# Attention in a two-layer decoder kernel: how the q and k operands of a head are rounded and placed, and where the norm's square stands

## The chip, the cores and the metric

The kernel runs on one core of a Trainium2 chip. The metric is the device time of one launch in microseconds (us). Five engines execute their own instruction streams in order and wait for one another by semaphores: TensorE (PE) multiplies matrices and transposes, VectorE (DVE) and ScalarE (ACT) do elementwise work and reductions, GpSimd (POOL) and SyncE (SP) are used here almost only to issue DMA transfers. Matmul results land in PSUM, in banks of 128 rows by 512 float32; everything else lies in SBUF.

## The reference

Two identical layers are applied to a residual stream x of 512 tokens by 1024 features, all float32:

```python
x = x + 0.5 * swiglu(rms_norm(x, ffn1_norm[l]), ffn1_w_in[l], ffn1_w_out[l])
h = rms_norm(x, mix_norm[l]) @ w_mix_in[l]
(c_x, c_b, c_c, h_q, h_f, h_i, h_g, f_q, f_k, f_v, f_f) = jnp.split(h, split_at, axis=-1)
y = jnp.concatenate([short_conv_mixer(c_x, c_b, c_c, conv_w[l]),
                     hgrn2_mixer(h_q, h_f, h_i, h_g, lower_bounds[l], hgrn_out_gain[l]),
                     fox_mixer(f_q, f_k, f_v, f_f, fox_f_bias[l], fox_q_gain[l], fox_k_gain[l])], axis=-1)
x = x + y @ w_mix_out[l]
x = x + 0.5 * swiglu(rms_norm(x, ffn2_norm[l]), ffn2_w_in[l], ffn2_w_out[l])
```

The change concerns fox_mixer, an attention of 8 heads of 64 features with normalised queries and keys and a forget term, and the last step of hgrn2_mixer:

```python
qh = rms_norm(heads(q), q_gain) * (HEAD_DIM ** -0.5)
kh = rms_norm(heads(k), k_gain)
cum = jnp.cumsum(jax.nn.log_sigmoid(f_logit + f_bias), axis=1)
s = jnp.einsum('bhqd,bhkd->bhqk', qb, kh) + (cb[..., :, None] - cum[..., None, :])   # causal mask
o = jnp.einsum('bhqk,bhkd->bhqd', softmax(s), vh)                                    # attention
o = rms_norm(o, out_gain) * silu(gate)                                               # end of hgrn2_mixer
```

## The kernel before

Each layer is a feed-forward stage, a mixing stage and a second feed-forward stage. In the feed-forward stages PE works through float32 products in three passes: every operand is split into a rounded high part and the remainder (ACT rounds, lines 311 and 803; DVE subtracts, lines 312 and 805), and lines 322, 330 and 331 multiply high by high, low by high and high by low. The same lines do the dense products of the mixing stage, with weights that SP loads (line 294). "Dense" below means these.

Attention goes head by head, 0 to 3 in the first half and 4 to 7 in the second. Function fox_prep makes the operands of one head. Four transposes bring q (64 rows) and k (64 rows) of the head into one bank. Then it forms four tiles for the score product: QA holds q high in rows 0 to 63 and q low in rows 64 to 127; KA holds k high in both halves; QB holds q high and two rows of ones; KB holds k low and two rows of the forget term. A product over the 128 rows of QA and KA gives high by high and low by high, and a second one over 66 rows of QB and KB gives high by low and the forget term. In the kernel before, ACT rounds q high into QA (line 1563) and k high into KA (line 1564), two transfers on SP copy q high to QB (line 1565) and k high to KA's other half (line 1566), and DVE subtracts to get q low (line 1567) and k low (line 1571), each operation over 64 rows. POOL writes the ones of QB in every call (line 1557). For heads 0 and 1 the transposes go to a bank of the kind "sc" before attention begins, for the others to one of the kind "pt". There are two banks of either kind.

Function fox_attend then walks through four blocks of 128 queries per head, in the order of items (h, i). `LOOK` = 3 items ahead it issues the scores (lines 1586 and 1587, a bank "sc"), DVE reduces them to the negated maximum nm (line 1591), ACT takes the exponential (line 274) and scales by the reciprocal of the sum (line 1597; for the third block DVE does, line 1599). At the item itself PE transposes P into a bank "pt" (line 1651), ACT rounds it to PH (line 1653), DVE forms the rest PL (line 1654), and one item later (`LAG` = 1) PE multiplies by V (line 1609). ACT and DVE then bring the result of a head from its bank "po" to fo (lines 1622 and 1623). The call for the next head's operands stands at the beginning of item (h, 0), so it is one head ahead; the second half is a new call of fox_attend, which begins with the operands of head 4.

Beside attention, PE gets dense work handed out in steps (the function beside in mix): the projections of the second half, the short convolution, then the output projection.

The hgrn2 mixer runs before attention in the same stage. Its final norm leaves a mean of squares in two pt banks. ACT takes Ln and Exp (through line 274) and a Square, and DVE combines this with the banks in two operations (line 1473, in0 = the bank): those are the last readers of the two banks. They stand in the instruction streams beside the first items of attention, whose transposes need the same two banks.

The order of the instructions on each engine isn't the order of the code: a scheduler lays them out by its own estimates and by priorities that rise in the order of the code. `high_priority()` makes the instructions issued within it go ahead of others that could stand at the same place.

Of the kernel before, what the change touches and what calls it, by code (L numbers as in the profile page):

```python
# [8 lines left out]
F32 = mybir.dt.float32  # L9
F32R = mybir.dt.float32r  # L10
# [3 lines left out]
AF = mybir.ActivationFunctionType  # L14
ALU = mybir.AluOpType
# [8 lines left out]
P = 128  # L24
# [20 lines left out]
EPS = 1e-6  # L45
# [3 lines left out]
NH = 8  # L49
# [108 lines left out]
class Trunk:  # L158
# [864 lines left out]
    def mix(self, l, w, w_out, conv_w, out_gain, q_gain, k_gain, f_bias, next_gain):  # L1023
        nc, tc = self.nc, self.tc
        FM2 = [slice(0, P), slice(P, 2 * P)]
        TOK = [slice(c, c + P) for c in (0, 128, 256, 384)]
        with tc.tile_pool(name=self.n("mix"), bufs=1) as mp:
# [10 lines left out]
            og, qkg, fb, cw = col("og", 1), col("qkg", 1), col("fb", NH), col("cw", 6)  # L1038
# [99 lines left out]
            for part, n in enumerate(hgrn):  # L1138
                if n is None:
                    break  # L1140
                if n == 0:
                    left.close()
                    ap1 = left.enter_context(
                        tc.tile_pool(name=self.n("at"), bufs=1, reuse_waits="tile")
                    )
                    for tag in ("PH", "PL"):
                        ap1.tile([P, 4, 2, P], F32R, tag=tag, name=self.n(tag), bufs=2)
                    ops = {h: self.fox_prep(ap1, h, half[0][0], qkg, "sc") for h in range(2)}
                if part < 2:
                    next(decay, None)  # L1150
                for _ in range(n):
                    next(dense, None)
            attend = self.fox_attend(ap1, 0, half[0], qkg, ops)
            next(attend)
            for _ in dense:
                pass
# [27 lines left out]
            def beside(attend, dense, first=0, then=()):  # L1184
                for _ in range(first):
                    next(dense, None)
                for n, _ in enumerate(attend, first):
                    if n == 3 and then:
                        then()
                    if n >= 2:  # L1190
                        next(dense, None)
                for _ in dense:
                    pass
# [23 lines left out]
                        add(2 * dg + i, banks[i])  # L1217

            beside(attend, conv(), 1, finish)
            beside(self.fox_attend(ap1, 1, half[1], qkg, {}), most())  # L1220
            self.ntog = 0
            for dg in range(2):
                banks = self.next4()
# [41 lines left out]
    def hgrn(self, l, hp, hb, z, q, v, sg, og):  # L1265
# [202 lines left out]
        for x in range(2):  # L1468
            self.act(span(r, x), mb[x], AF.Ln, bias=self.epsc)
        self.act(r, r, AF.Exp, scale=-0.5)  # L1470
        self.act(t, r, AF.Square)
        for x in range(2):
            nc.vector.scalar_tensor_tensor(
                out=span(t, x), in0=mb[x], scalar=EPS, in1=span(t, x), op0=ALU.add, op1=ALU.mult
            )
        nc.vector.tensor_scalar(t, t, scalar1=-0.5, scalar2=1.5, op0=ALU.mult, op1=ALU.add)
        nc.vector.tensor_mul(r, r, t)
        nc.vector.tensor_mul(o, o, r)
# [70 lines left out]
                )  # L1549
        half[hf] = qk, V  # L1550

    def fox_prep(self, pool, h, qk, g, tag="pt"):
        nc = self.nc
        tl = lambda p, tag: pool.tile([p, T], F32R, tag=tag, name=self.n(tag), bufs=2)
        QA, QB, KA, KB = tl(P, "QA"), tl(66, "QB"), tl(P, "KA"), tl(66, "KB")
        nc.sync.dma_start(KB[64:66, :].bitcast(F32), self.negc[h : h + 1, :, :].bitcast(F32))
        nc.gpsimd.memset(QB[64:66, :].bitcast(F32), 1.0)
        b = self.bank(tag)
        for i in range(4):
            nc.tensor.transpose(  # L1560
                b[:, i * P : (i + 1) * P], qk[:, i, h % 4].rearrange("p w d -> p (w d)"), self.ident
            )
        nc.scalar.activation(QA[:64, :], b[:64, :], AF.Copy, scale=g[:64, :])
        nc.scalar.activation(KA[64:, :], b[64:, :], AF.Copy, scale=g[64:, :])
        nc.sync.dma_start(QB[:64, :].bitcast(F32), QA[:64, :].bitcast(F32))
        nc.sync.dma_start(KA[:64, :].bitcast(F32), KA[64:, :].bitcast(F32))
        nc.vector.scalar_tensor_tensor(
            out=QA[64:, :], in0=b[:64, :], scalar=g[:64, :], in1=QA[:64, :],
            op0=ALU.mult, op1=ALU.subtract,
        )  # L1570
        nc.vector.scalar_tensor_tensor(
            out=KB[:64, :], in0=b[64:, :], scalar=g[64:, :], in1=KA[64:, :],
            op0=ALU.mult, op1=ALU.subtract,
        )
        return QA, QB, KA, KB

    def fox_attend(self, pool, hf, qkv, g, ops):
        nc = self.nc
        qk, V = qkv
        tl = lambda tag, n: pool.tile([P, T], F32, tag=tag, name=self.n(tag), bufs=n)  # L1580

        def scores(ops, i):
# [46 lines left out]
        late = []  # L1629
        heads = range(4 * hf, 4 * hf + 4)  # L1630
        items = [(h, i) for h in heads for i in range(4)]
        if heads[0] not in ops:
            ops[heads[0]] = self.fox_prep(pool, heads[0], qk, g)
        pb = {it: scores(ops[heads[0]], it[1]) for it in items[:LOOK]}
        for n, (h, i) in enumerate(items):
            yield
            if i == 0 and h + 1 in heads and h + 1 not in ops:
                ops[h + 1] = self.fox_prep(pool, h + 1, qk, g)
            if n + LOOK < len(items):
                h2, i2 = items[n + LOOK]  # L1640
                pb[h2, i2] = scores(ops[h2], i2)
# [10 lines left out]
            t3 = tb.rearrange("p (j t) -> p j t", j=4)[:, : i + 1, :]  # L1652
            nc.scalar.copy(PH[:, : i + 1, i % 2, :], t3)
            nc.vector.tensor_sub(PL[:, : i + 1, i % 2, :], t3, PH[:, : i + 1, i % 2, :])
            if len(late) and n >= late[0][0] + LAG:
                values(*late.pop(0)[1:])
            if i % 2:
# [215 lines left out]
```

## Time and profile before

Three runs took 1806.88, 1807.59 and 1808.02 us.

| | |
|---|---|
| median of the three runs | 1807.59 us |
| profiled execution | 1808.44 us |
| its span | 1806.7 us |
| granted TensorE clock in it | 1.0 |
| instructions in the trace | 34748 |
| attention stage, first layer | about 450 to 590 us of the span |
| attention stage, second layer | about 1340 to 1480 us |
| feed-forward stages | 50 to 340, 590 to 900, 900 to 1240 and 1480 to 1807 us |

A table by stage gives, for a stretch of the span, its length and then the busy time of PE, of PE's weight loads, of DVE, ACT and POOL, each with the number of instructions, then the clock, the share of the DMA engines' time and GB/s. A list of waits names the engine, tile and line that waited, the engine, tile and line that released it, the total in us, the number of times and the longest. A line of the timeline holds start, duration, engine, line, operation, the tiles written and read, and in brackets the idle time of the engine just before it and what ended this. A line on a group gives count, then least, median and greatest duration in ns. PE's instructions overlap: the distance from one start to the next is what one costs.

### The profile page before, as it was taken

The numbers are of one execution on the slowest core, as the hardware profiler recorded it, in microseconds if no ns is written. First come the engines' busy times: TensorE is split into PE (matmuls) and PEld (weight loads), VectorE is DVE, ScalarE is ACT, GpSimd is POOL, SyncE is SP. The second block draws the span as 40 slices with busy tenths as digits, with TensorE's granted clock in tenths as the row PEclk, the third lists the DMA queues.
The fourth block names the chain that finished last, engine by engine and source line by source line (L and its number), as shares of the span: only waits on it lengthen the run. The fifth ranks groups of instructions, "written<-read, shape, count | busy, mean of one in ns | idle before, by whom it ended". The sixth has DMA issues, their size and how long they took to land.

```text
span 1806.7 us, 34748 instructions
## 1 busy us (share of the span) xinstructions
PE 1795.8 (99%) x14267; PEld 1681.3 (93%) x14267; DVE 1453.4 (80%) x2036; ACT 1000.7 (55%) x1437; POOL 170.4 (9%) x172
## 2 busy tenths in 40 slices
PE   9999999999999999999999999999999999999999
PEld 7899999899888899999889999998998888999997
DVE  8889787776887898879679887876868878888893
ACT  5455554464786465556446555555547855555551
POOL 0011120100000001112001111201000000020210
PEclk9999999999999999999999999999999999999999
DMA  7668783233323767868265787823333247687762
GB/s 203 182 142 186 178 178 98 72 79 83 88 74 111 218 140 161 198 160 169 82 205 133 165 189 191 169 66 81 78 89 89 71 138 188 164 159 192 159 134 94
DMA packets 243486, 250.94 MB, mean 139 GB/s; under 512 B 18520, under 2 KB 228192, under 8 KB 243328
## 3 DMA queue, kind: packets, MB, share of 16 engines
q1 hardware_dynamic: 189424, 182.38, 33.8%
q0 software_dynamic: 53600, 66.09, 23.2%
q8 instruction: 112, 1.84, 0.4%
q14 instruction: 46, 0.38, 0.1%
q10 hardware_dynamic: 304, 0.27, 0.0%
HBM read 223.98 MB, written 2.10 MB: 125 GB/s over the span
## 4 chain that ended last, share of the span: by engine, by line
PE 92%; DVE 3%; ACT 3%; issue 1%; DMA 1%; SPq 0%; ACTq 0%; DVEq 0%
PE mm L322 13%; PE mm L330 13%; PE mm L331 13%; PE sc L330 6%; PE sc L331 6%; PE sc L322 6%; PE pt L322 6%; PE pt L330 6%; PE pt L331 6%; PE po L330 4%; PE po L322 4%; PE po L331 4%; ACT hl L311 1%; PE po L1609 1%; PE pt L1651 1%
## 5 line engine op out<-in xcount | busy, mean ns | idle before, releaser
L803 ACT CAST hl<-w 128x1024 fp32r<-128x1024 f32 x322 | 336.7, 1050 | 313.7 <-PE mm L331 82.4
L805 DVE TENSOR_TENSOR hl<-w,hl 128x1024 fp32r<-128x1024 f32 x322 | 392.2, 1221 | 80.7 <-ACT hl L803 80.7
L312 DVE TENSOR_TENSOR hl<-st,hl 128x512 fp32r<-128x512 f32 (+3 forms) x192 | 162.3, 845 | 106.3 <-ACT hl L311 105.5
L311 ACT CAST hl<-st 128x512 fp32r<-128x512 f32 (+3 forms) x192 | 142.6, 743 | 169.9 <-PE po L331 64.6
L322 PE MATMUL mm<-xc,hl 128*128 128x256 f32 (+1 forms) x733 | 201.2, 276 | 0.0
L330 PE MATMUL mm<-xc,hl 128*128 128x256 f32 x728 | 201.2, 276 | 0.0
L331 PE MATMUL mm<-xc,hl 128*128 128x256 f32 x728 | 201.0, 276 | 0.0
L322 PE MATMUL sc<-xc,hl 128*128 128x256 f32 (+1 forms) x532 | 146.0, 276 | 0.0
L330 PE MATMUL sc<-xc,hl 128*128 128x256 f32 x528 | 146.0, 276 | 0.0
L331 PE MATMUL sc<-xc,hl 128*128 128x256 f32 x528 | 145.9, 276 | 0.0
L322 PEld LDWEIGHTS mm<-xc,hl 128*128 128x128 f32 x733 | 137.4, 188 | 0.2
L330 PEld LDWEIGHTS mm<-xc,hl 128*128 128x128 f32 x728 | 136.7, 188 | 0.0
L331 PEld LDWEIGHTS mm<-xc,hl 128*128 128x128 f32 x728 | 136.7, 188 | 0.0
L322 PE MATMUL pt<-xc,hl 128*128 128x256 f32 (+1 forms) x482 | 132.6, 276 | 0.0
L330 PE MATMUL pt<-xc,hl 128*128 128x256 f32 x480 | 132.6, 276 | 0.0
L331 PE MATMUL pt<-xc,hl 128*128 128x256 f32 x480 | 132.5, 276 | 0.0
L322 PE MATMUL mm<-x,hl 128*128 128x512 f32 x272 | 107.4, 395 | 0.0
L331 PE MATMUL mm<-x,hl 128*128 128x512 f32 x272 | 106.4, 391 | 0.0
L330 PE MATMUL mm<-x,hl 128*128 128x512 f32 x272 | 106.1, 390 | 0.0
L322 PEld LDWEIGHTS sc<-xc,hl 128*128 128x128 f32 x532 | 99.7, 188 | 0.2
L331 PEld LDWEIGHTS sc<-xc,hl 128*128 128x128 f32 x528 | 99.1, 188 | 0.1
L330 PEld LDWEIGHTS sc<-xc,hl 128*128 128x128 f32 x528 | 99.2, 188 | 0.0
(513 smaller groups left out, 5594.1 us busy)
## 6 DMA issues: line engine op xcount, KB each, us to landing
w<-in_ffn_w_in_dram SPq DMA_DIRECT2D x140, 512.0 KB
w<-in_ffn_w_out_dram SPq DMA_DIRECT2D x64, 512.0 KB
w<-in_ffn_w_out_dram POOLq DMA_DIRECT2D x56, 512.0 KB, 8.3
st<-in_w_mix_in_dram SPq DMA_DIRECT2D x88, 256.0 KB
st<-in_ffn_w_in_dram SPq DMA_DIRECT2D x70, 256.0 KB
w<-in_ffn_w_in_dram POOLq DMA_DIRECT2D x35, 512.0 KB, 8.5
w<-S POOLq DMA_DIRECT2D x35, 512.0 KB, 4.7
st<-in_ffn_w_out_dram SPq DMA_DIRECT2D x24, 512.0 KB
```

The costliest lines, as they stand in the source:

```text
L311: a = nc.scalar.copy(hi, src[:, c : c + w])
L312: b = nc.vector.tensor_sub(lo, src[:, c : c + w], hi)
L322: i = nc.tensor.matmul(acc[:, c], ah, bh[:, c], start=first and c.start == 0, stop=False, skip_group_check=True,)
L330: nc.tensor.matmul(acc, a, b, start=False, stop=False, skip_group_check=True)
L331: i = nc.tensor.matmul(acc, c, d, start=False, stop=last, skip_group_check=True)
L803: A(nc.scalar.copy(hi, src))
L805: return lambda: V(nc.vector.tensor_sub(lo, src, hi))
L1609: nc.tensor.matmul(self.ob[:, t0 + u * P : t0 + 2 * P], V[:, j, h % 4].rearrange("p a d -> p (a d)"), part[:, j, u:, :].rearrange("p i t - ...
L1651: nc.tensor.transpose(tb[:, j * P : (j + 1) * P], p[:, j * P : (j + 1) * P], self.ident)
```

## The change

It has three parts.

First, fox_prep gets a second form, `ahead=True`, for heads 2 to 7. One ACT operation over all 128 rows rounds the bank into KA (q high in rows 0 to 63, k high in rows 64 to 127), and one DVE operation over 128 rows writes the remainders into QA (q low above, k low below). Four transfers on POOL's queue then place the halves: KA's upper half to QB, QA's lower half to KB, KA's upper half to QA's lower half, and at last KA's lower half to its upper half. To make this so, the order of halves in QA is turned: q low in rows 0 to 63, q high in rows 64 to 127. The third transfer overwrites what the second reads; the fourth overwrites what the first and the third read. Heads 0 and 1 keep the old form.

Second, these operands are made two heads ahead: the call stands behind the rounding of item (h, 0) and is for head h + 2, across the two halves too, so that heads 4 and 5 are prepared in the first half. QB is no longer a new tile per head but one of two lasting ones, whose rows of ones are written once per layer.

Third, the Square of the hgrn norm and the two DVE operations that read the banks stand in `high_priority()`.

PE at the beginning of attention in the first layer. Before: the scores of head 0's last and head 1's first block, the first transpose of P, then dense work.

```order
L1586 MATMUL sc_5471<-KA_5286,QA_5284 128x512
L1587 MATMUL sc_5471<-KB_5287,QB_5285 128x512
L1586 MATMUL sc_5487<-KA_5303,QA_5301 128x128
L1587 MATMUL sc_5487<-KB_5304,QB_5302 128x128
L1651 MATMUL pt_5483<-ident,P_5387 128x128
L322 MATMUL mm_5451<-x_383_3562,hl_5505 128x512
```

PE at the same place after (line 1565 is now the transposes of fox_prep, 1603 and 1604 the scores, 1664 the transposes of P).

```order
L1603 MATMUL sc_5471<-KA_5289,QA_5288 128x512
L1604 MATMUL sc_5471<-KB_5290,QB_5284 128x512
L1664 MATMUL pt_5483<-ident,P_5387 128x128
L1565 MATMUL pt_5491<-ident,qk_4135 128x128 x4
L1603 MATMUL sc_5502<-KA_5304,QA_5303 128x128
L1604 MATMUL sc_5502<-KB_5305,QB_5285 128x128
L322 MATMUL mm_5451<-x_383_3562,hl_5520 128x512
```

The transposes for head 2 now stand directly behind the first transpose of P, and take the second pt bank. The dense matmuls follow behind the scores.

DVE at that place before. T_5544 is the norm's tile, pt_5376 and pt_5377 are its two banks; V is the values' tile of the second half.

```order
L1599 TENSOR_SCALAR P_5407<-P_5407,rs_5406 128x384
L312 TENSOR_TENSOR hl_5573<-st_5570,hl_5573 128x512
L1546 SCALAR_TENSOR_TENSOR V_5246<-mm_5247,invc_3890,V_5246 128x4x64
L1546 SCALAR_TENSOR_TENSOR V_5246<-po_5248,invc_3890,V_5246 128x4x64
L1473 SCALAR_TENSOR_TENSOR T_5544<-pt_5376,T_5544 128x512
L1546 SCALAR_TENSOR_TENSOR V_5246<-mm_5247,invc_3890,V_5246 128x4x64
L312 TENSOR_TENSOR hl_5608<-st_5605,hl_5608 128x512
L1546 SCALAR_TENSOR_TENSOR V_5246<-po_5248,invc_3890,V_5246 128x4x64
L1591 ISA P_5476,nm_5474<-sc_5471,zm_3700 128x512
L1591 ISA nm_5474 128x1
L1654 TENSOR_TENSOR PL_5482<-pt_5483,PH_5481 128x128
L1473 SCALAR_TENSOR_TENSOR T_5544<-pt_5377,T_5544 128x512
```

DVE there after (line 1477 is the former 1473, 1551 the former 1546).

```order
L1612 RECIPROCAL rs_5396<-rs_5396 128x1
L1477 SCALAR_TENSOR_TENSOR T_5559<-pt_5376,T_5559 128x512
L312 TENSOR_TENSOR hl_5588<-st_5585,hl_5588 128x512
L1477 SCALAR_TENSOR_TENSOR T_5559<-pt_5377,T_5559 128x512
L1612 RECIPROCAL rs_5406<-rs_5406 128x1
L1551 SCALAR_TENSOR_TENSOR V_5246<-mm_5247,invc_3890,V_5246 128x4x64
L1616 TENSOR_SCALAR P_5407<-P_5407,rs_5406 128x384
L1551 SCALAR_TENSOR_TENSOR V_5246<-po_5248,invc_3890,V_5246 128x4x64
L312 TENSOR_TENSOR hl_5623<-st_5620,hl_5623 128x512
L1551 SCALAR_TENSOR_TENSOR V_5246<-mm_5247,invc_3890,V_5246 128x4x64
L1608 ISA P_5476,nm_5474<-sc_5471,zm_3700 128x512
```

The two readers of the norm's banks have moved up, ahead of the V operations and the third block's scaling, and only one hl subtraction parts them.

SP around the seam between the halves, before: the transfers of heads 4 and 5 stand between the weight loads (numbers 6064 to 6067 belong to head 4, 6111 to 6114 to head 5).

```order
L294 DMA st_6327<-in_w_mix_out_dram 128x2x256
L294 DMA st_6367<-in_w_mix_out_dram 128x256
L1565 DMA QB_6065<-QA_6064 64x512
L1566 DMA KA_6066<-KA_6066 64x512
L1565 DMA QB_6112<-QA_6111 64x512
L1566 DMA KA_6113<-KA_6113 64x512
L294 DMA st_6399<-in_w_mix_out_dram 128x2x256
```

POOL after, for head 5 (6013 to 6015) and the first of head 6 (6137).

```order
L1578 DMA QB_5285<-KA_6014 64x512
L1578 DMA KB_6015<-QA_6013 64x512
L1578 DMA QA_6013<-KA_6014 64x512
L1578 DMA KA_6014<-KA_6014 64x512
L1578 DMA QB_5284<-KA_6137 64x512
```

The copies have gone from SP to POOL, where nothing else stands between them in this stage.

PE at the seam, after: the last scores of head 4, the transposes of head 6, four dense matmuls, and the first scores of head 5. The transposes of head 5 stand 50 rows ahead of the last two rows.

```order
L1603 MATMUL sc_6120<-KA_5837,QA_5836 128x512
L1604 MATMUL sc_6120<-KB_5838,QB_5284 128x512
L1664 MATMUL pt_6132<-ident,P_6095 128x128
L1565 MATMUL pt_6140<-ident,qk_4812 128x128 x4
L322 MATMUL mm_6166<-cyh_3698,hl_6210 128x512
L330 MATMUL mm_6166<-cyl_6043,hl_6210 128x512
L331 MATMUL mm_6166<-cyh_3698,hl_6210 128x512
L322 MATMUL mm_6167<-cyh_3698,hl_6210 128x512
L1603 MATMUL sc_6151<-KA_6014,QA_6013 128x128
L1604 MATMUL sc_6151<-KB_6015,QB_5285 128x128
```

Before, the operands of heads 4 and 5 were made here, at the seam; now those of head 6 are.

The diff:

```diff
@@ mix
+                    self.qb = pair(ap1, "QB", F32R)
+                    for t in self.qb:
+                        nc.gpsimd.memset(t[64:66, :].bitcast(F32), 1.0)
                     ops = {h: self.fox_prep(ap1, h, half[0][0], qkg, "sc") for h in range(2)}
...
-            attend = self.fox_attend(ap1, 0, half[0], qkg, ops)
+            attend = self.fox_attend(ap1, 0, half, qkg, ops)
...
-            beside(self.fox_attend(ap1, 1, half[1], qkg, {}), most())
+            beside(self.fox_attend(ap1, 1, half, qkg, ops), most())
@@ hgrn
-        self.act(t, r, AF.Square)
-        for x in range(2):
-            nc.vector.scalar_tensor_tensor(
-                out=span(t, x), in0=mb[x], scalar=EPS, in1=span(t, x), op0=ALU.add, op1=ALU.mult
-            )
+        with self.tc.high_priority():
+            self.act(t, r, AF.Square)
+            for x in range(2):
+                nc.vector.scalar_tensor_tensor(
+                    out=span(t, x), in0=mb[x], scalar=EPS, in1=span(t, x),
+                    op0=ALU.add, op1=ALU.mult,
+                )
@@ fox_prep
-    def fox_prep(self, pool, h, qk, g, tag="pt"):
+    def fox_prep(self, pool, h, qk, g, tag="pt", ahead=False):
...
-        QA, QB, KA, KB = tl(P, "QA"), tl(66, "QB"), tl(P, "KA"), tl(66, "KB")
+        QA, KA, KB = tl(P, "QA"), tl(P, "KA"), tl(66, "KB")
+        QB = self.qb[h % 2][:66, :]
         nc.sync.dma_start(KB[64:66, :].bitcast(F32), self.negc[h : h + 1, :, :].bitcast(F32))
-        nc.gpsimd.memset(QB[64:66, :].bitcast(F32), 1.0)
...
+        if ahead:
+            f = lambda a, r=slice(0, 64): a[r, :].bitcast(F32)
+            k = slice(64, P)
+            nc.scalar.activation(KA, b, AF.Copy, scale=g)
+            nc.vector.scalar_tensor_tensor(
+                out=QA, in0=b, scalar=g, in1=KA, op0=ALU.mult, op1=ALU.subtract
+            )
+            for out, src in (
+                (f(QB), f(KA)), (f(KB), f(QA, k)), (f(QA, k), f(KA)), (f(KA), f(KA, k)),
+            ):
+                nc.gpsimd.dma_start(out, src)
+            return QA, QB, KA, KB
@@ fox_attend
-        if heads[0] not in ops:
-            ops[heads[0]] = self.fox_prep(pool, heads[0], qk, g)
...
-            if i == 0 and h + 1 in heads and h + 1 not in ops:
-                ops[h + 1] = self.fox_prep(pool, h + 1, qk, g)
...
             nc.vector.tensor_sub(PL[:, : i + 1, i % 2, :], t3, PH[:, : i + 1, i % 2, :])
+            if i == 0 and h + 2 < NH:
+                ops[h + 2] = self.fox_prep(
+                    pool, h + 2, half[(h + 2) // 4][0], g, ahead=True
+                )
```

More of the change, by code (lines that the diff above doesn't have):

```diff
@@ L1575, in fox_prep, with fox_attend @@
         return QA, QB, KA, KB
-    def fox_attend(self, pool, hf, qkv, g, ops):
+    def fox_attend(self, pool, hf, half, g, ops):
         nc = self.nc
-        qk, V = qkv
+        V = half[hf][1]
         tl = lambda tag, n: pool.tile([P, T], F32, tag=tag, name=self.n(tag), bufs=n)
```

## The prediction

> **What bounds the kernel now.** I read the table of busy time first, then the chain that ended last, then the busy time by stage.
>
> ```profile
> PE 1795.8 (99%) x14267; PEld 1681.3 (93%) x14267; DVE 1453.4 (80%) x2036; ACT 1000.7 (55%) x1437; POOL 170.4 (9%) x172
> PE 92%; DVE 3%; ACT 3%; issue 1%; DMA 1%; SPq 0%; ACTq 0%; DVEq 0%
> ...
> 50.00:340.00 290.00, 290.00 (x2290) 279.27 (x2289) 236.20 (x260) 151.24 (x178) 34.43 (x29) 1.00 0.65 151
> 450.00:590.00 140.00, 137.15 (x825) 115.62 (x825) 117.64 (x264) 103.31 (x220) 4.15 (x8) 1.00 0.32 89
> 1340.00:1480.00 140.00, 137.40 (x838) 116.20 (x838) 115.72 (x262) 101.64 (x218) 4.14 (x8) 1.00 0.33 91
> ```
>
> TensorE (PE) is busy for 99% of the span and carries 92% of the chain. In a feed-forward stage (50 to 340 us) it has no idle time at all. The change touches only the two attention stages (450 to 590 and 1340 to 1480 us; after the length come the busy times of PE, weight load, DVE, ACT and POOL, the clock, the DMA share and GB/s). There PE is idle 140 - 137.15 = 2.85 us and 140 - 137.40 = 2.60 us. The change leaves PE's instructions as they are in number, so what is visible to win is 5.45 us, 0.3% of the time; to lose there is no such limit, because PE executes in order and a late operand stops everything behind it. The clock is 1.00 throughout and plays no part. Of PE's waits over the whole kernel, these lie in the two stages (total, times, longest):
>
> ```profile
> PE pt L1651 <- DVE T L1473: 2.6, 2, 1.5
> ...
> PE po L1609 <- ACT PH L1653: 0.8, 2, 0.4
> PE sc L1586 <- DVE nm L1591: 0.7, 2, 0.4
> PE pt L1651 <- DVE KB L1571: 0.4, 2, 0.2
> ...
> PE sc L1586 <- DVE fo L1623: 0.2, 1, 0.2
> PE po L1609 <- DVE PL L1654: 0.2, 1, 0.2
> ```
>
> Nothing of the SP queue is among them, so moving SP's transfers away can win nothing directly.
>
> **The norm with priority.** The largest wait stands at the first transposes of attention: they need a pt bank, which the norm's last two DVE operations (L1473) still read.
>
> ```profile
> 466.77 1.04 ACT L274 ACTIVATE T<-T 128x1024 f32<-128x1024 f32 x1
> 467.72 0.79 ACT L1597 ACTIVATE P<-P,rs 128x128 f32<-128x128 f32 x2
> 468.41 0.60 ACT L274 ACTIVATE P<-P,nm 128x384 f32<-128x384 f32 x1
> 469.01 0.61 ACT L311 CAST hl<-st 128x512 fp32r<-128x512 f32 x1
> 470.25 1.05 ACT L274 ACTIVATE T<-T 128x1024 f32<-128x1024 f32 x1
> ...
> 469.68 0.69 DVE L312 TENSOR_TENSOR hl<-st,hl 128x512 fp32r<-128x512 f32 x1
> 471.33 0.69 DVE L1473 SCALAR_TENSOR_TENSOR T<-pt,T 128x512 f32<-128x512 f32 x1 [0.18 <-ACT T L274]
> 474.13 0.68 DVE L1473 SCALAR_TENSOR_TENSOR T<-pt,T 128x512 f32<-128x512 f32 x1
> ...
> 470.27 0.28 PE L1587 MATMUL sc<-KB,QB 66*128 66x128 f32 x1
> 472.08 0.33 PE L1651 MATMUL pt<-ident,P 128*128 128x128 f32 x1 [1.53 <-DVE T L1473]
> ```
>
> The norm's Exp ends at 467.8. ACT then does two scalings of P, one Exp of a P, one rounding, and only at 470.25 the norm's Square; the first bank comes free at 472.0. With priority the Square stands behind at most one of these scalings: it starts at about 468.2 and ends at 469.2, and the first L1477 ends at 469.9, before PE arrives at 470.5. That wait, 1.53 us here and 2.6 - 1.5 = 1.1 in the other layer, goes. It doesn't go whole. In the new order the four transposes of head 2 stand directly behind the first transpose of P and need the second bank. Its reader is parted from the first one by one hl subtraction, so it runs from 469.9 + 0.7 = 470.6 to 471.3; PE is there at about 470.6: 0.7 us of wait. I put the same at 0.2 in the other layer, where the wait of before was 0.4 shorter. Then the next transposed block waits for one DVE operation more (the QA of head 2, a 128x512 operation like the 0.69 above): 0.6 in each layer, partly beside the two dense matmuls. Gain: 2.6 - 0.7 - 0.2 - 0.6 = 1.1, bounds 0 and 2.6.
>
> **The operands of a head.** Durations of the four operations that a head costs now, and of the memset (min/median/max ns):
>
> ```profile
> L1563 ACT ACTIVATE QA<-pt,qkg x12: 670/680/684, 484.4 to 1437.9; 64x512 fp32r<-64x512 f32 x12
> L1564 ACT ACTIVATE KA<-pt,qkg x12: 682/683/685, 485.1 to 1438.6; 64x512 fp32r<-64x512 f32 x12
> L1567 DVE SCALAR_TENSOR_TENSOR QA<-pt,qkg,QA x12: 743/744/745, 486.3 to 1439.4; 64x512 fp32r<-64x512 f32 x12
> L1571 DVE SCALAR_TENSOR_TENSOR KB<-pt,qkg,KA x12: 754/755/758, 487.0 to 1440.2; 64x512 fp32r<-64x512 f32 x12
> L1557 POOL MEMSET QB<- x16: 518/521/545, 455.4 to 1424.8; 2x512 f32 x16
> ```
>
> One ACT and one DVE operation of 128 rows replace two and two of 64 rows. The DVE rows of 128x512 above (0.68 and 0.69) are no longer than those of 64x512, so I price the new pair at 0.68 and 0.74. Each of heads 2 to 7 saves 0.68 us on ACT and 0.75 on DVE, 4.1 and 4.5 us a layer. That is worth no time by itself: both engines are off the path, ACT busy 103.31 of 140 us and DVE 117.64. What it removes on PE is the wait on L1571 above, 0.4 in all, since the bank is read by two operations and no longer four. Six memsets fewer per layer (0.52 each, on POOL, 4.15 us busy in 140) cost and win nothing. That heads 4 and 5 are prepared before the seam removes the wait of the restart (on nm, 0.32 and 0.38), but brings new ones: the third block of head 3 needs the bank that the QA of head 5 reads, and the first block of head 4 finds ACT busy with that head's Exp. Each is between 0 and 0.9; I take the seam as 0, bounds -0.7 and +1.8 over both layers.
>
> **The transfers.** This is the step with a price that before doesn't show. Before, two independent transfers go out on SP. After, four go out on POOL, and three of them are a chain: KB from QA's lower half (waits for DVE), then QA's lower half from KA (overwrites what the former read), then KA's upper half from its lower (overwrites what that one read). Every transfer behind a waiting one on POOL waits too; POOL has nothing else to do there, so nobody but the head itself is delayed. On SP two issues per head go; what stood behind them, the weight loads of line 294, starts earlier, and PE waits for none of it now.
>
> ```profile
> 521.20 0.49 SPq L1565 DMA_DIRECT2D QB<-QA  x1
> 521.88 0.47 SPq L1566 DMA_DIRECT2D KA<-KA  x1
> 524.40 0.22 PE L1586 MATMUL sc<-KA,QA 128*128 128x128 f32 x1
> ...
> og<-in_hgrn_out_gain_dram POOLq DMA_DIRECT2D x4, 0.2 KB, 2.2
> ...
> fb<-in_fox_f_bias_dram POOLq DMA_DIRECT2D x2, 4.0 KB, 2.9
> ...
> w<-S POOLq DMA_DIRECT2D x35, 512.0 KB, 4.7
> ```
>
> The second SP transfer (128 KB) is issued at 521.88 and its reader starts at 524.40 with no wait shown, so that it lands within 2.5 us. From POOL the rows give 2.2 us (0.2 KB), 2.9 (4 KB from DRAM) and 4.7 (512 KB, which also accumulates). A copy of 128 KB inside SBUF is nearest to the SP transfer in size and place and to the small ones in queue; I take 2.5, bounds 2.2 and 4.7. [...]
>
> When is the chain needed? The tightest place is head 5. In the new order its transposes stand behind the first transpose of P of head 3, and 50 rows of PE later, its first score.
>
> ```profile
> 514.36 0.27 PE L1651 MATMUL pt<-ident,P 128*128 128x128 f32 x1
> ...
> 514.94 0.25 ACT L1653 CAST PH<-pt 128x128 fp32r<-128x128 f32 x1
> ...
> 485.06 0.39 PE L331 MATMUL mm<-x,hl 128*128 128x512 f32 x1
> 485.29 0.40 PE L322 MATMUL mm<-x,hl 128*128 128x512 f32 x1
> ...
> 482.60 0.60 PE L1560 MATMUL pt<-ident,qk 128*128 128x128 f32 x4
> 482.96 0.48 PE L1586 MATMUL sc<-KA,QA 128*128 128x512 f32 x1
> ```
>
> From these rows: PH ends at 515.19, KA (0.68) at 515.87, QA (0.74) at 516.6. The chain then lands at 516.6 + 3 x 2.5 = 524.1. PE starts a matmul of 512 columns every 0.23 us and a 128-wide transpose every 0.09 (four in 0.36). Between 514.36 and the first score of head 5 stand 16 dense matmuls (3.7), 20 value matmuls (14 of 256 and 6 of 128 columns, 2.15), 19 transposes (1.7) and 8 score matmuls (1.2): 8.75 us, so PE comes at 523.1, or 524.1 with the waits of the seam. The wait is 0 to 1.0; I take 0.4.
>
> Head 6 follows on its heels. Its QA stands 27 DVE operations behind that of head 5, which is 12.0 us at this stage's mean (117.64/264 = 0.45 each) and 9.3 at the closest pace:
>
> ```profile
> 530.00:540.00 10.00, 9.88 (x61) 7.99 (x61) 9.20 (x29) 9.36 (x25) 0.52 (x1) 1.00 0.25 66
> ```
>
> (29 operations in 10 us, before.) Between the two I take 10.9: QA ends at 527.5, the chain at 535.0. Its first score stands 53 rows of PE behind that of head 5, 10.1 us by the same prices: 523.1 + 0.4 + 10.1 = 533.6, and 534.2 with 0.6 for the blocks of P in between, whose reductions stand behind that QA on DVE. Wait 0.8, bounds 0 and 2. The other heads have 15 to 18 us between transposes and first score. So 1.2 us a layer, 2.4 in all. Bounds: 0 (landing 2.2), and with 4.7 a landing at 530.7, 7 us a layer. Before, this place costs nothing, as the row at 524.40 shows.
>
> **The sum.** -1.1 (norm) - 0.4 (KB) + 0 (seam) + 2.4 (chain) = +0.9 us. The profiled execution took 1808.44 us (span 1806.7 and 1.7 around it), 0.85 above the median 1807.59 of the runs; against the median the forecast is 1808.5.
>
> **Rivals.** First, the chain is late: a landing of 3.5 us makes it 10.5, head 5's operands at 527.1 against PE at about 523.6, 3.5 us, and 0.5 more at head 6, whose chain also grows: 1807.6 - 1.5 + 8.0 = 1814.1, slower. It decides from about 2.9 us on, where the two heads wait 2.55 us a layer (these eat the 1.5 gained and 3.6 more, 0.2% of the time, which is about what a measurement can tell from no change). For it speak 2.9 for 4 KB and 4.7 for 512 KB; against it, the SP copy of the same bytes in under 2.5 and the 2.2.
>
> Second, DVE and ACT, relieved by 8.6 us a layer, also end the other waits: all 5.45 us of idle PE go, 1802.1, faster. Against it: what is left of the waits (on PH, PL, nm, fo) are short chains from one operation to its reader, not backlogs.
>
> Third, the change does nothing that shows: the norm's wait only moves on to the second bank and the seam, the chain is hidden: 1807.6.
>
> Fourth, POOL is slowed while DVE is at work. Its issues in the feed-forward stages, with DVE busy 236.20 of 290 us, don't show it:
>
> ```profile
> L820 POOL DMA_DIRECT2D w<-S x35: 877/887/899, 74.5 to 1737.2; - x35
> ```
>
> They lie within 22 ns of one another. If each issue of the chain had to wait out one DVE operation of 0.69, a landing would be 3.2 and head 5's chain at 526.2: 2.6 us there and 0.6 at head 6, 1807.6 - 1.5 + 6.4 = 1812.5, slower. [...]
>
> **Chances.** Forecast 0.48, chain late 0.27, all waits gone 0.11, nothing 0.08, POOL slowed 0.06. Faster by over 0.2% (3.6 us) takes the second rival and a small tail of the forecast: 0.13. Slower takes the first and most of the fourth: 0.32. The rest, 0.55, is within 0.2%. The range goes from 1803.8 (most of the visible idle time gone) to 1813.5 (a landing of 3.3 us); the forecast's own is 1806.3 to 1810.7 (the chain at 0.1 to 2.3 us a layer).
>
> **What would show it.** Right: no wait of PE on the norm's operation at the first transposes, or one under 0.8; none on its successor to KB; first scores of heads 5 and 6 that wait about 0.4 and 0.8 us for a transfer, and none of the other heads; landings of line 1578 near 2.5; DVE busy about 4.5 us less in each attention stage. Wrong: landings over 2.9 us, with PE's waits at line 1603 put down to KA's transfer; or a list of PE waits in the attention stages that adds up to under 1 us.

## The result, and the profile after

In runs side by side the changed kernel took 1811.27 us (median of 17, 1808.54 to 1814.03), the kernel before 1807.47 (median of 17). The ratio is 1.0019, with a 95% interval of 1.0012 to 1.0026: slower by 0.19%. The interval lies above 1, so the loss is real, and it is just within the 0.2% that the prediction set as the border of no change. The forecast was 1808.5 in a range of 1803.8 to 1813.5, with a narrower range of its own of 1806.3 to 1810.7.

The changed kernel's profiled execution took 1813.08 us with a span of 1811.3. Its busy times:

```profile
PE 1797.1 (99%) x14267; PEld 1684.2 (93%) x14267; DVE 1443.1 (80%) x2024; ACT 993.1 (55%) x1425; POOL 189.2 (10%) x208
```

Its list of PE's waits (total, times, longest), as far as they lie in the attention stages:

```profile
PE sc L1603 <- DMA KA<-KA: 4.4, 2, 4.2
PE pt L1664 <- DVE PL L1667: 1.3, 4, 0.4
...
PE po L1626 <- ACT PH L1666: 0.8, 2, 0.4
PE pt L1565 <- DVE T L1477: 0.5, 1, 0.5
```

The two attention stages, by the columns shown before:

```profile
450.00:590.00 140.00, 138.44 (x837) 117.78 (x836) 113.92 (x260) 101.06 (x216) 13.60 (x26) 1.00 0.37 101
...
1340.00:1480.00 140.00, 134.00 (x810) 114.11 (x809) 106.06 (x249) 95.28 (x207) 13.60 (x26) 0.98 0.35 95
```

The first layer's stage did what a gain looks like: PE's idle time fell from 2.85 to 1.56 us. The second layer's rose from 2.60 to 6.00, and the clock there is 0.98, no longer 1.00. The new first entry of the list says why: one wait of 4.2 us for the last transfer of a head's chain.

Both profiles hold 14267 matmul records, nearly all in the same order, so the start of the matmul with the same number can be compared. Between the beginning and the end of a stage the changed kernel gained 1.86 us on the one before in the first layer. In the second it gained 1.0 us up to head 5 and lost 6.55 around the first score of head 6, 5.6 in all. The sum, 3.7 us, is the measured difference of the medians, 3.8.

The place itself, in the timeline of the changed kernel: the three chained transfers of head 6 in the first layer (its start, then the issue's duration), and the first score of head 6; and the same in the second layer.

```profile
528.09 0.52 POOL L1578 DMA_DIRECT2D KB<-QA  x1 [0.27 <-DVE nm L1608]
531.02 0.52 POOL L1578 DMA_DIRECT2D QA<-KA  x1 [2.40 <-DMA KB<-QA]
533.48 0.52 POOL L1578 DMA_DIRECT2D KA<-KA  x1 [1.94 <-DMA QA<-KA]
535.89 0.30 PE L1603 MATMUL sc<-KA,QA 128*128 128x128 f32 x1 [0.19 <-DMA KA<-KA]
...
1419.58 0.52 POOL L1578 DMA_DIRECT2D KB<-QA  x1 [0.26 <-DVE nm L1608]
1423.53 0.52 POOL L1578 DMA_DIRECT2D QA<-KA  x1 [3.43 <-DMA KB<-QA]
1428.16 0.52 POOL L1578 DMA_DIRECT2D KA<-KA  x1 [4.11 <-DMA QA<-KA]
1431.42 0.44 PE L1603 MATMUL sc<-KA,QA 128*128 128x128 f32 x1 [4.21 <-DMA KA<-KA]
```

In the first layer the steps of the chain are 2.93, 2.46 and 2.4 us, and PE, which arrives as the last one lands, waits 0.19. In the second layer the same steps take 3.95, 4.63 and 3.26: 11.8 us in place of 7.8, and all 4 us of it are waited for. The order leaves this place no slack, so each late landing is paid for in full.

The wait isn't the whole price. The clock behind it, by stretches of the changed kernel, and then two of the dense matmuls there in its timeline:

```profile
1427.00:1430.00 3.00, 0.20 (x1) 0.00 (x0) 0.69 (x1) 0.78 (x2) 1.55 (x3) 1.00 0.24 66
1430.00:1431.00 1.00, 0.00 (x0) 0.00 (x0) 0.00 (x0) 0.00 (x0) 0.00 (x0) 0.73 0.94 245
1431.00:1437.00 6.00, 5.58 (x15) 4.55 (x16) 0.80 (x4) 0.98 (x4) 1.04 (x2) 0.50 0.24 57
1437.00:1438.00 1.00, 1.00 (x10) 1.00 (x10) 0.28 (x1) 0.81 (x2) 0.00 (x0) 0.86 0.01 0
1438.00:1441.00 3.00, 3.00 (x17) 2.56 (x17) 3.00 (x9) 2.18 (x6) 0.00 (x0) 1.00 0.27 85
```

```profile
1433.26 0.63 PE L330 MATMUL mm<-cyl,hl 128*128 128x512 f32 x1
1433.68 0.63 PE L331 MATMUL mm<-cyh,hl 128*128 128x512 f32 x1
```

PE idles, the granted clock drops to 0.50 for some 6.8 us (half of the stretch at 0.73, all of the next, and 0.3 us of the one at 0.86), and the matmuls that follow start 0.43 us apart, where 0.23 was usual. Eleven of them at 0.2 us more are nearly all of the other 2.3 us: 4.2 + 2.3 = 6.5. The lowered clock wasn't an accident of one execution: the mean clock was 0.998 or 0.999 in all 17 runs of the changed kernel.

### The profile page after: what moved, and what is told of

It reads as the page before. It is cut to its first block, busy times and chain, and to the rows that moved or that the text cites. A ratio compares the mean times of both kernels' runs of the same rounds, so it can differ in the third digit from the quotient of the medians.

```text
span 1811.3 us, 34728 instructions
## 1 busy us (share of the span) xinstructions
PE 1797.1 (99%) x14267; PEld 1684.2 (93%) x14267; DVE 1443.1 (80%) x2024; ACT 993.1 (55%) x1425; POOL 189.2 (10%) x208
## 4 chain that ended last, share of the span: by engine, by line
PE 90%; ACT 3%; DVE 3%; DMA 2%; issue 1%; SPq 0%; POOL 0%; ACTq 0%; DVEq 0%; POOLq 0%
PE mm L322 13%; PE mm L330 13%; PE mm L331 13%; PE sc L322 6%; PE sc L330 6%; PE sc L331 6%; PE pt L322 6%; PE pt L330 6%; PE pt L331 6%; PE po L330 3%; PE po L322 3%; PE po L331 3%; DMA st<-in_ffn_w_in_dram 1%; PE po L1626 1%; DMA st<-in_w_mix_in_dram 1%
```

## The experiments

Each experiment was timed beside the kernel before (11 or 12 executions, e8 only 5), in three sessions: e1 to e4, e5 to e7, e8 to e10. The kernel before had medians of 1807.18, 1807.33 and 1806.84 in them, so a difference of half a microsecond between kernels of different sessions says nothing. "By stage" below is the shift of matmuls with the same number between the beginning and the end of an attention stage, against the profile of before, in the first and second layer; it leaves out the first 100 us of the span, in which a run shifts by up to a microsecond and more. A negative shift is a gain.

| kernel | median us | ratio to before, 95% interval | mean clock of its runs | by stage |
|---|---|---|---|---|
| changed kernel | 1811.27 | 1.0019 (1.0012 to 1.0026) | 0.998 to 0.999 | -1.86, +5.60 |
| e1, norm alone | 1806.10 | 0.9995 (0.9986 to 1.0003) | 1.000 | -0.96, -0.60 |
| e2, transfers on SP | 1804.66 | 0.9986 (0.9977 to 0.9994) | 1.000 | -1.75, -1.44 |
| e3, old form, two ahead | 1809.11 | 1.0012 (1.0003 to 1.0021) | 1.000 | +0.62, +0.70 |
| e4, no priority | 1809.65 | 1.0014 (1.0003 to 1.0025) | 0.998 to 1.000 | -1.35, +0.04 |
| e5, chain of two, POOL | 1804.01 | 0.9982 (0.9973 to 0.9991) | 1.000 | -2.24, -1.46 |
| e6, chain of four, POOL | 1809.33 | 1.0014 (1.0005 to 1.0023) | 0.998 to 1.000 | -1.26, +3.19 |
| e7, chain of two, SP | 1803.26 | 0.9980 (0.9971 to 0.9989) | 1.000 | -2.13, -1.78 |
| e8, double loads | 1814.61 | 1.0041 (1.0029 to 1.0054) | 0.997 to 0.999 | +6.26, +3.79 |
| e9, e7 without priority | 1804.01 | 0.9986 (0.9977 to 0.9995) | 1.000, one run 0.999 | -1.85, -1.41 |
| e10, e7 one head ahead | 1808.31 | 1.0007 (0.9999 to 1.0016) | 1.000 | -0.22, +1.19 |

### e1: the norm's priority alone

```diff
 (kernel before)
+        with self.tc.high_priority():
             self.act(t, r, AF.Square)
             for x in range(2):
                 nc.vector.scalar_tensor_tensor(...)
```

> The kernel before with the norm's priority alone. Theory A (what the changed kernel lost is the late chain of POOL transfers at head 6, 4.2 us in the second layer, and TensorE's clock at half for some us behind it; the other two parts win): the wait of 2.6 us on the norm's banks shrinks to about 0.5, some of it comes back elsewhere, no transfer is waited for, clock 1.000: 1806.0 to 1807.0. Theory B (the new order of the work beside the norm and at the seam costs by itself): 1807.5 or more, with new waits of PE in its place.

1806.10, in the range of theory A, though the interval of the ratio includes 1, so that the gain shows clearly only by stage (1.56 us). The wait on the norm's operation is gone from the list, and the one on L1573, which is the former L1571, has grown from 0.4 to 0.8.

### e2: the same transfers on SP's queue

```diff
 (changed kernel)
-                nc.gpsimd.dma_start(out, src)
+                nc.sync.dma_start(out, src)
```

> The changed kernel with its four transfers issued by SP instead of POOL, everything else in the same order. Theory A: each copy lands in 2.0 to 2.5 us instead of 2.5 to 4.2, the chain of head 6 takes 6 to 7.5 us instead of 11.9, PE waits for it under 1 us or not at all and the clock stays at 1.000: 1804.5 to 1806.5. Rival: the waits of the chain now hold SP's weight loads behind them, PE waits for hl, and the time stays above 1809. Theory B: 1809 or more, with the waits of PE on transposes and P unchanged.

1804.66: 6.6 us less than the changed kernel (6.3 when each is set against the kernel before of its own session), from the change of queue alone; ACT and DVE keep their order, and PE's differs by four dense rows. PE's waits for P and for a transfer in e2's list, and then, in its timeline, the transfers of head 6 in the second layer:

```profile
PE pt L1664 <- DVE PL L1667: 1.9, 4, 0.6
...
PE sc L1603 <- DMA KA<-KA: 0.4, 1, 0.4
```

```profile
1417.30 0.46 SPq L1578 DMA_DIRECT2D KB<-QA  x1
1420.12 0.46 SPq L1578 DMA_DIRECT2D QA<-KA  x1
1422.40 0.49 SPq L1578 DMA_DIRECT2D KA<-KA  x1
```

The steps are 2.82 and 2.28, where POOL's took 3.95 and 4.63. Over the whole trace the steps from KB to QA and from QA to KA have a median of 2.7 us in e2 and go up to 3.6; in the changed kernel these are 2.9 and 4.6. PE's wait for them is 0.4 in the whole kernel, and the clock stays at 1.000. SP now waits in the chain with weight loads behind it, as the rival had it, but PE waits for none of them: its list has no entry for hl, and the wait on zf stands in the list of before too. Theory A holds. The run doesn't part a quicker queue from the loads that are now held back behind the copies.

### e3: the old operations, two heads ahead

```diff
 (changed kernel)
                 ops[h + 2] = self.fox_prep(
-                    pool, h + 2, half[(h + 2) // 4][0], g, ahead=True
+                    pool, h + 2, half[(h + 2) // 4][0], g
                 )
```

> The changed kernel with the old form of operands (two ACT and two DVE operations of 64 rows, two independent transfers on SP) for heads 2 to 7, still two heads ahead and with the norm's priority. Theory A: no chain of transfers, so no wait at head 6 and no half clock: 1804.5 to 1806.5, the two visible attention stages with about 1.6 us of idle PE each. Theory B (placing the work two heads ahead costs): 1809 or more.

1809.11, a miss: no late chain, a clock of 1.000, and yet slower than before. The list of PE's waits:

```profile
PE pt L1664 <- DVE KB L1588: 1.9, 4, 0.5
...
PE po L1626 <- DVE PL L1667: 1.1, 2, 0.6
```

At the new place, behind the rounding of item (h, 0), the operands' bank is wanted again by the third block's transposes. Two ACT and two DVE operations hold it longer than one of each: 1.9 us of waiting on the last of them, and 1.1 for the values behind. So the 128-row form, which I had priced at no time because ACT and DVE are off the path, is worth 4.4 us at this place (e3 against e2, both with SP's transfers; 4.5 by stage). The list points to how long a bank is held, not to how busy the engines are, but it doesn't account for the whole: PE's idle time in the two stages is 4.94 us in e3 and 3.89 in e2. A wait counts as idle only from the end of the matmul before it, which is modelled, so part of a delay doesn't show there. That the bank is the reason for all 4.4 us is argued, not shown.

### e4: no priority for the norm

```diff
 (changed kernel)
-        with self.tc.high_priority():
-            self.act(t, r, AF.Square)
-            ...
+        self.act(t, r, AF.Square)
+        ...
```

> The changed kernel without the norm's priority. Theory A: the wait on the norm's banks is back, 1 to 2.6 us over both layers, and the wait at head 6 stays: 1812 to 1814. If the priority only moved work about (theory B): the same as the changed kernel, 1811.3, or less.

1809.65, below the range of theory A and, by the number alone, on the side of theory B; but it is a mixture. The 12 runs spread from 1805.72 to 1816.64. The runs with a mean clock of 1.000 (7) have a median of 1807.63; the five with 0.998 or 0.999 took 1810.02 to 1816.64. In its profiled execution, the shortest with 1805.72 us, the wait on the norm's banks is back (2.4 us), the wait for KA is 1.3 and the clock stays at 1.00. So the lowered clock comes and goes from run to run, and whether it comes sets the time more than the norm's place does. That it is the late chain each time is likely, but one profile can't show it. What the priority is worth had to be asked where no chain is late (e9).

### e5: the chain cut to two, still on POOL

```diff
 (changed kernel)
             for out, src in (
-                (f(QB), f(KA)), (f(KB), f(QA, k)), (f(QA, k), f(KA)), (f(KA), f(KA, k)),
+                (f(QB), f(KA)), (f(KB), f(QA, k)), (f(KA), f(KA, k)), (f(QA, k), f(QB)),
             ):
```

QA's lower half now comes from QB, so that KA may be overwritten without waiting for it. The number of transfers and the result are the same.

> The changed kernel, still with four transfers on POOL, but with the chain cut from three to two: QA's lower half is copied from QB in place of KA, and KA's upper half is overwritten as soon as QB is copied. Theory A (length of the chain of landings decides): head 6's operands come some 3 us earlier, PE waits there 0 to 1 us in either layer, the clock stays at 1.000 in most runs: 1804.5 to 1807. Rival (any transfer on POOL's queue is late by chance, whatever the chain): still above 1809, clock 0.998 to 0.999. In the new order PE's scores of a few heads stand some rows earlier, which takes part of the gain.

1804.01, half a microsecond under the expected range and below the kernel before with the whole interval, and no run with a lowered clock. POOL's last three transfers of head 6 in the second layer, and PE's one wait for a transfer that is left:

```profile
1417.04 0.52 POOL L1578 DMA_DIRECT2D KB<-QA  x1 [0.27 <-DVE nm L1608]
1420.36 0.52 POOL L1578 DMA_DIRECT2D KA<-KA  x1 [2.79 <-issue]
1421.28 0.67 POOL L1578 DMA_DIRECT2D QA<-QB  x1 [0.40 <-issue]
...
1424.58 0.30 PE L1603 MATMUL sc<-KA,QA 128*128 128x128 f32 x1 [0.36 <-DMA QA<-QB]
```

From KB's issue to PE's first score are 7.5 us, where the chain of three took 11.8. POOL's landings are no quicker (QA, which waits for KB, is issued 4.2 us after it); there is one fewer to wait for. Queue and length are thus two remedies for one cause: the sum of landings behind the last DVE operation.

### e6: the chain made longer

```diff
 (changed kernel)
-                (f(QA, k), f(KA)), (f(KA), f(KA, k)),
+                (f(QA, k), f(KA)), (f(QA, k), f(KA)), (f(KA), f(KA, k)),
```

> The changed kernel with the third transfer made twice, a chain of four landings. Theory A: 2.5 to 4 us more until the operands of heads 5 and 6 are there. The order of PE puts their scores some rows later, about 1 to 2 us; so 1 to 3 us more wait at each of the four places, and the clock at half for some us behind each wait of over 2 us: 1815 to 1830. Rival (the wait in the second layer is one late landing by chance, not the chain's length): within 2 us of the changed kernel.

1809.33: a miss in the other direction, between medians 2 us faster than the chain of three, though the two intervals overlap. The scheduler counts the transfer. It put the first scores of heads 5 and 6 12 rows of PE (13 matmuls) later, which is about one landing. Two of PE's waits in the second layer of e6, at heads 2 and 6, and then the clock around the first of them:

```profile
1378.60 0.33 PE L1604 MATMUL sc<-KA,QA 128*128 128x128 f32 x1 [1.68 <-DMA KA<-KA]
...
1432.60 0.30 PE L1604 MATMUL sc<-KA,QA 128*128 128x128 f32 x1 [1.33 <-DMA KA<-KA]
```

```profile
1376.00:1379.00 3.00, 1.32 (x8) 0.82 (x7) 1.63 (x4) 1.51 (x4) 0.52 (x1) 1.00 0.77 205
...
1380.00:1382.00 2.00, 2.00 (x6) 1.52 (x6) 1.61 (x5) 1.20 (x4) 0.31 (x1) 0.50 0.53 107
...
1383.00:1386.00 3.00, 3.00 (x19) 2.62 (x19) 1.70 (x5) 1.64 (x4) 0.52 (x1) 1.00 0.21 46
```

The expectation's 2 us, as the wait behind which the clock is halved, was an estimate that no run shows: here the clock is 0.50 behind a wait of 1.68, and it is 1.00 from 1430 to 1440, around the wait of 1.33.

So "longer chain, longer wait" was too simple: what PE waits is the chain less the distance that the order leaves, and the scheduler sets that distance from the chain it sees. For the chain of three the distance covered steps of 2.4 to 2.9 us, with nothing over for steps of 4.

### e7: both remedies

e5's order of transfers, with `nc.sync.dma_start`.

> Both remedies: the chain of two, on SP. Theory A: no wait of PE for a transfer, clock 1.000; against the chain of three on SP (1804.7) there is only one wait of 0.4 us left to win: 1803.5 to 1805. Rival: SP's queue, with the transfer of KA now waiting ahead of the one of QA, holds weight loads longer and costs 1 us or more.

1803.26, the fastest and 0.2 us under the expected range: 0.9980 of the kernel before, with no wait for a transfer in the list.

### e8: weight loads doubled

```diff
 (changed kernel)
-            d = nc.sync.dma_start(s3[:, :, at : at + w], ap.rearrange("(k p) c -> p k c", p=P))
+            for _ in range(getattr(self, "loads", 1)):
+                d = nc.sync.dma_start(s3[:, :, at : at + w], ap.rearrange("(k p) c -> p k c", p=P))
...
+            self.loads = 2
             beside(self.fox_attend(ap1, 1, half, qkg, ops), most())
+            self.loads = 1
```

> The changed kernel with SP's weight loads of the second half of attention made twice each (the same bytes into the same place); the order of PE and POOL is unchanged. Theory C (the copies on POOL land late, 3.5 to 4.6 us in place of 2.7, where a weight load of 256 KB is under way): nearly every copy of heads 6 and 7 meets a load, PE's wait for KA grows at head 6 in both layers, clock 0.998 or lower: 1813 to 1820. Rival (POOL's queue is late by itself, loads don't matter): 1810 to 1812.5. Should PE wait for hl instead, the loads themselves were late, and the run says nothing on this.

1814.61, inside theory C's range, but not at the place that it named. The list of PE's waits:

```profile
PE pt L1667 <- DVE PL L1670: 3.2, 4, 1.3
PE sc L1606 <- DMA KA<-KA: 2.4, 2, 1.7
PE sc L1606 <- DVE fyl L1647: 2.2, 1, 2.2
PE po L1629 <- ACT PH L1669: 2.1, 3, 1.2
```

The 2.2 us that the list puts down to fyl are another wait for a transfer: it stands before the first score of head 5, which reads KA and QA and nothing of fyl. That score and the last copy before it, in the first layer and then in the second:

```profile
522.81 0.52 POOL L1581 DMA_DIRECT2D KA<-KA  x1 [2.61 <-issue]
525.73 0.45 PE L1606 MATMUL sc<-KA,QA 128*128 128x128 f32 x1 [2.16 <-DVE fyl L1647]
...
1422.72 0.52 POOL L1581 DMA_DIRECT2D KA<-KA  x1 [2.54 <-issue]
1425.10 0.30 PE L1606 MATMUL sc<-KA,QA 128*128 128x128 f32 x1 [1.65 <-DMA KA<-KA]
```

So PE waits 4.6 us for transfers, at head 5 in both layers and at head 6 in the second. From the issue of KB to the first score of head 5 are 10.1 and 9.6 us; in the changed kernel it is about 8 in both layers, and no wait. This speaks for theory C, at head 5 in place of heads 6 and 7, and in a single profiled execution, the longest of the five. The rest of the loss is another matter: PE waits 3.2 us for DVE's PL and 2.1 for ACT's PH, by the list above, against 1.3 and 0.8 in the changed kernel. That both engines stood behind weights that came late is my reading; it isn't shown.

### e9: e7 without the priority, and e10: e7 one head ahead

e9 takes `high_priority()` out of e7. e10 puts the calls of fox_prep back where the kernel before has them (for h + 1 at the start of item (h, 0), for head 4 at the start of the second half), with the new operations and the chain of two on SP.

> The chain of two on SP, without the norm's priority. With no late chain to swallow it, the priority is worth what the kernel before with it alone won, 1.0 to 1.5 us: 1804.3 to 1805.2, against 1803.3 with it. Rival: in the new order the priority is worth nothing: 1803.3.

1804.01, under the expected 1804.3 to 1805.2 and above the rival's 1803.3. It is 0.75 us above e7 between medians of two sessions, which isn't clear of the noise, and 0.65 by stage. Its wait on the norm's banks is 2.3 us, yet only 0.65 is won by removing it: the rest comes back at the following blocks.

> The chain of two on SP with the norm's priority, but operands made one head ahead, where the kernel before makes them. If making them two heads ahead is worth something by itself, the seam shows: the restart of the second half and the scores of heads 4 and 6 wait, 1 to 4 us in all: 1804.5 to 1807. Rival: the 128-row operations and the short chain are the whole gain: 1803 to 1804.

1808.31, 5 us above e7 and outside both ranges, on the slow side. PE's wait list of e10 begins with

```profile
PE sc L1603 <- DMA QA<-QB: 3.4, 5, 1.0
```

Five waits for transfers, of up to 1.0 us: one head ahead, even a chain of two on SP isn't hidden. The two heads' distance isn't worth something at the seam alone, it is what makes a chain of transfers affordable.

## Why the prediction was right, and where it wasn't

The time lies in the range, and the sign was right. The sum came out at +0.9 us and the medians at +3.8, for two terms that were both too small and of opposite sign; that it came this near is partly luck. The time lies outside the forecast's own narrower range, on the side of the first rival. Of the signs that the prediction named, the norm's came as forecast, but its sign of being wrong came too: landings over 2.9 us, with PE's wait at line 1603 put down to KA's transfer.

**The norm.** Right in kind. The two operations stand where I put them, 469.38 and 470.59 in the changed kernel against my 469.2 and 470.6:

```profile
469.38 0.69 DVE L1477 SCALAR_TENSOR_TENSOR T<-pt,T 128x512 f32<-128x512 f32 x1 [2.02 <-ACT T L274]
469.99 0.68 DVE L312 TENSOR_TENSOR hl<-st,hl 128x512 fp32r<-128x512 f32 x1
470.59 0.68 DVE L1477 SCALAR_TENSOR_TENSOR T<-pt,T 128x512 f32<-128x512 f32 x1
```

The wait for the second bank is 0.5 in one layer (forecast 0.7 and 0.2), the next block waits some 0.3 in each (forecast 0.6). Alone the priority won 1.1 us between medians (forecast 1.1), beside the rest 0.75, neither clear of the noise; by stage 1.56 and 0.65.

**The operands.** "That is worth no time by itself" is the step that failed on the side of the gain. ACT and DVE are off the path on average, but the bank that their operations hold is not; e3 against e2 measures 4.4 us at the new place, of which the lists show a part. The 0.4 us for KB and 0 for the seam were part of that picture: PE's waits on KB and on nm are gone, and waits on PL of 0.25 to 0.4 have come. In the stage of the first layer, where the chain cost 0.19, the forecast without the chain was -0.75 a layer; it measured about -2.0.

**The transfers.** The mechanism, the place and the typical price were right: head 6, a chain of three, PE there as the last one lands. Its QA ends at 527.80 (forecast 527.5), its chain at 535.8 (535.0), and head 5's first score, at 524.16, comes without a wait. The landings of all the transfers, and their issues, in the changed kernel:

```profile
L1578 POOL DMA_DIRECT2D KB<-QA x12: 522/522/538, 475.6 to 1429.2; - x12
...
DMA to landing us min/median/max: 2.2/2.6/4.2
```

The median of 2.6 is the 2.5 that I took. The step that failed is "the chain then lands at 516.6 + 3 x 2.5": one landing for all. The copies of head 6 landed in 2.6, 2.2 and 2.3 us in the first layer and in 3.0, 3.9 and 3.1 in the second; together with 1.1 us more between a landing and POOL's next issue, that made 11.8 us of 7.8. The term was 2.4 us; it measured about 6.7 in the profiled execution (0.2 and 6.5), and 7.3 between the medians of the changed kernel and of e5.

**The clock.** "The clock is 1.00 throughout and plays no part" was read from before and held only for it. In the changed kernel's second layer it was 0.50 for some 6.8 us, and a wait of 4.2 us cost 6.5. No term of the sum had this.

**The rivals.** "The chain is late" is what happened, in one layer out of two in the profile, and at head 6, where the rival had most of it at head 5. "All waits gone", 1802.1, is by its number nearly what e7 reaches once the chain is short (1803.26), though PE still idles 3.1 us in e7's two stages. POOL slowed by DVE is not seen: the issues above lie within 16 ns of one another, and from KB's issue at head 6 on DVE runs the same operations at the same distances in both layers, to 0.01 us over 7.8 us, so it can't make one chain 7.8 us and the other 11.8. The transfers that SP issues are quicker in the traces, with a median of 2.7 us a step in e2 against 2.9 in the changed kernel, and no run here shows that DVE is the reason.

**Open.** Why POOL's steps took 4 us in the second layer at head 6. SP issues the same loads at the same distances from KB's issue in both layers. But the copy to QA is issued 0.9 us ahead of SP's next load in the first layer (531.02 and 531.92) and 0.1 us behind it in the second (1423.53 and 1423.41). Late landings go with SP's traffic all over this trace. Of the 22 copies that no other copy overlaps, 12 have at most 0.2 MB of SP's loads moving beside them and land in 2.16 to 2.38 us; 10 have a whole load of 0.26 MB beside them and land in 2.40 to 3.87. e8 points the same way. The prediction let SP's loads start earlier and gave that no price. What made the first step a microsecond late, and why a whole load costs one copy 0.2 us and another 1.7, stays open, and no run takes the loads away with all else equal.

## What to carry to other kernels

A chain of dependent transfers has to be priced at the sum of its landings at their late end (11.8 us here), not at their median (7.8), and it costs nothing only if the order leaves that much distance: shorten the chain first (copy from a place that nobody overwrites), then choose the queue. Work that is off the critical path on an engine can still sit on the path through the buffer that it holds (4.4 us between e3 and e2, of which the lists show a part). And price a wait of PE at more than its length where the clock falls with it: here it was 0.50 for some 6.8 us, and 4.2 us of waiting cost 6.5.

## What the runs showed of the hardware that I hadn't expected

The clock fell after shorter gaps than I would have thought. In e6 a single wait of 1.68 us, with 1.68 of the 3.0 us around it idle, is followed by 0.50 for some 3.4 us (the clock is 0.74 from 1379 to 1380, 0.50 to 1382, 0.55 to 1383 and 1.00 again from there), while a wait of 1.33 in the same stage, one of 1.33 in e4 and the 1.53 of the kernel before left it at 1.00. With the 4.2 us of the changed kernel it stayed at 0.50 for twice as long, some 6.8 us. The longest single gap alone doesn't tell these cases apart: in e8 the clock was 1.00 from 550 to 556 us and 0.57 from 556 to 560, behind a wait of 1.24 us with another of 0.57 within a microsecond. What decides when it falls and when it comes back isn't shown by these runs. Across the runs of e4, those with a mean clock below 1.000 took 1810.02 us and more, against a median of 1807.63 of the others.
